# Moved matmuls in the output projection and the expert layer, and the last sums started from two fp32r terms

## The chip, the cores and the metric

The kernel runs on one core of a Trainium2 chip. The core's engines run their own instruction streams side by side: TensorE (PE in the rows; PEld are its weight loads), VectorE (DVE), ScalarE (ACT), GpSimd (POOL) and SyncE (SP, which here only issues DMAs). The metric is the device time of one execution in microseconds (us); several executions are timed and the median is taken.

## The reference

One layer of a decoder trunk on 512 tokens of width 1024, in float32: a token mixer (attention, pooling and state-space branches, merged and projected), a layer norm, then 32 experts of which each token uses two, and a second layer norm. Cut to the parts that the change touches:

```python
def layer_norm(h, g, b, eps=1e-5):
    mu = jnp.mean(hf, -1, keepdims=True)
    var = jnp.mean(jnp.square(hf - mu), -1, keepdims=True)
    return ((hf - mu) * lax.rsqrt(var + eps)).astype(h.dtype) * g + b

def moe_ffn(x, w_grp, b_grp, w_exp, b_exp, w_gate, w_up, w_down):
    p_grp = jax.nn.softmax((xf @ w_grp + b_grp).astype(jnp.float32), -1)
    ...
    w_top, e_top = lax.top_k(p_in, MOE_TOPK)
    ...
    def expert_block(args):
        xb, e = args
        h = jax.nn.silu(xb @ w_gate[e]) * (xb @ w_up[e])
        return h @ w_down[e]

    ys = lax.map(expert_block, (xs, blk_e)).reshape(P, D)
    out = jax.ops.segment_sum(ys * buf_w[:, None].astype(ys.dtype), buf_t, num_segments=T)

def reference(x, w_in, ...):
        mix = token_mixer(x, w_in[l], ...)      # ends in merged @ w_out
        x = layer_norm(DN_ALPHA * x + mix, ln1_g[l], ln1_b[l])
        ffn = moe_ffn(x, router_w_grp[l], ...)
        x = layer_norm(DN_ALPHA * x + ffn, ln2_g[l], ln2_b[l])
```

## The kernel before

The 512 tokens are four tiles `tt` of 128 rows. `out_proj` (from about 515 us) multiplies the merged branches by `w_out`, 512 output columns (a half) at a time: a first half with all four tiles (96 matmuls of `mm3`, lines 70 to 72, each fp32 product made of three fp32r ones), then for each tile the second half, the transposition of its rows (`transpose_rows`, line 1055), the norm and the routing. Inside it `router_consts` folds the norm's gain and bias into the router's weights: VectorE sums products of the router's weights with `gb`, which is loaded on ScalarE's queue (line 927), into `wsum`, and TensorE adds these over the partitions with one matmul against ones (line 938).

`moe` (from 595 us) then goes through the 32 experts in order. An expert's weights are 6 MB, in six pieces of 1 MB: two for gate, two for up, two for down. SyncE loads them (`load_piece`, line 1439) in the order gate(e), up(e), down(e-1), into a ring of 20 buffers; a piece is issued when the program order reaches it and its buffer's last reader is done. For each expert TensorE does 32 matmuls of gate and up (`gate_up`, line 1355) into one bank `mm`; `hidden` (lines 1364 to 1366) makes `th` of them on ScalarE and VectorE; `turn` transposes `th` of the expert before (line 1374) between gate and up, and `flush` calls `down` (line 1387) for it, whose result is cast and subtracted (lines 1391, 1393) into a high and a low fp32r part `y`. After each odd expert, `gather_turn` (line 1342) turns the next pair's rows and `combine` adds the pair's outputs, by 16 matmuls with a selection matrix `ot` (lines 1408, 1409; four per tile) and 8 additions on VectorE (line 1418), to `acc`, which begins as the norm's output times a constant (`residual`). `route_further` and `further_slots` work out slots for tokens beyond an expert's 64; they are wanted by `overflow`, a loop on the chip that stands ahead of expert 16 and runs as often as there are further blocks. Ahead of it, weights are loaded up to 13 pieces past the start of expert 16.

At the end, `start_tile` puts `acc` into the last sums' banks with a matmul against the identity, the last pair's outputs are added in the same banks, and `final` takes norms from them (line 1592) and writes the output. Most of TensorE's instructions are pinned in program order (`inorder`); the others are placed by a scheduler.

Of the kernel before, what the change touches and what calls it, by code (L numbers as in the profile page):

```python
# [18 lines left out]
S = 512  # L19
# [24 lines left out]
class Build:  # L44
# [869 lines left out]
    def router_consts(self, p):  # L914
# [22 lines left out]
        ps = self.bank("o")  # L937
        nc.tensor.matmul(ps[:, 0:72], ones, sm.rearrange("p i n -> p (i n)"), start=True, stop=True)
        nsg = p.tile([128, 36], F32, name="nsg")
        nc.vector.tensor_scalar(nsg, ps[:, 0:36], -1.0, None, op0=OP.mult)  # L940
        V(br, br, ps[:, 36:72], OP.add)
        return wr, nsg, br

    def out_proj(self, mh, ml):
# [11 lines left out]
        rc = self.router_consts(p)  # L956
# [16 lines left out]
        for tt in range(NT):  # L973
            evac(0, tt, accs[tt])

# [106 lines left out]

    def residual(self, t, c):

        nc = self.nc
        cs = slice(c * 512, (c + 1) * 512)
        for i, nm in enumerate(("ln1_g", "ln1_b")):
            nc.scalar.dma_start(t[:, i], dram(self.I[nm], c * 512, [[0, 128], [1, 512]]))
        nc.scalar.mul(t, t, ALPHA)
        for tt in range(NT):  # L1090
            r = self.acc[tt // 2][:, tt % 2, cs]
            self.tc.keep_in_program_order(nc.vector.tensor_tensor(r, r, t[:, 0], OP.mult))
            nc.vector.tensor_tensor(r, r, t[:, 1], OP.add)
# [215 lines left out]
    def further_slots(self, part):  # L1309
# [4 lines left out]
        if part == 0:  # L1314
            self.fps = self.bank("pt")[0:64, 0:32]
        for tt in (part * 2, part * 2 + 1):
            for i in range(2):
# [6 lines left out]
                self.inorder(nc.tensor.matmul(self.fps, rk, wo.rearrange("p a n -> p (a n)"), start=(tt == 0 and i == 0),  # L1324
                                              stop=(tt == NT - 1 and i == 1)))
        if part:
            T(self.idxo, self.fps[:, 0:16], 4096.0, None, op0=OP.add)
            for h in range(2):
                T(self.wt48[h * 64:(h + 1) * 64, 32:48], self.fps[:, 16:32], 0.5, None, op0=OP.mult)
# [81 lines left out]
    def combine(self):  # L1411

        for tt in range(NT):
            for dh in range(2):
                ps = self.bank("s" if tt % 2 else "pt")
# [3 lines left out]
        self.terms = []  # L1419
# [32 lines left out]
    def moe(self):  # L1452
        p = self.ep
# [18 lines left out]
        for e in range(E):  # L1472
            pr, odd = e // 2, e % 2
            if pr == LOOP and not odd:
# [10 lines left out]
            hT = []  # L1485
            gu = self.gate_up(xq[:, :, odd * 64:(odd + 1) * 64], self.pieces(e, 0), self.pieces(e, 1),
                              (lambda: hT.append(self.turn(pend[1]))) if pend and e > 1 else None)
            if e == 0:
                self.load_until(len(self.first))
                fetch(1, xs1)  # L1490
                self.slot_weights()
                pend = (0, self.hidden(gu, self.wt48[:, 0:1]), None)
                continue
# [3 lines left out]
            if e == 2:  # L1497
                self.slots_everywhere()
                self.further_slots(0)
                pend = (*pend[:2], self.slot_rows(self.sid[:, 0:1]))  # L1500
# [4 lines left out]
            if odd:  # L1505
# [5 lines left out]
                if self.terms:  # L1511
                    self.combine()
# [3 lines left out]
            if e == 1:  # L1516
                srt = self.route_further()
            if e == 2:
                self.further_slots(1)
                srt.close()  # L1520
            if e in (1, 2):
                self.residual(gb, e - 1)
            if odd and pr:
                ot = self.slot_rows(self.sid[:, pr:pr + 1], t=self.moe_tile() if end else None)
            pend = (e, th, ot if odd and pr else None)
        self.ahead = [self.start_tile(tt) for tt in range(2)]
        self.flush(pend, self.turn(pend[1]))
# [3 lines left out]
    def start_tile(self, tt):  # L1531

        halves = [self.bank(t) for t in (("s", "s"), ("mm", "mm"), ("mm", "pt"), ("pt", "o"))[tt]]
        for dh in range(2):
            self.nc.tensor.matmul(halves[dh], self.ident, self.acc[tt // 2][:, tt % 2, dh * 512:(dh + 1) * 512], start=True, stop=False)  # L1535
        return halves

# [222 lines left out]
```

## Time and profile before

| | us |
|---|---|
| median of 3 runs (1094.75 to 1098.54) | 1097.99 |
| the profiled execution | 1097.79 |
| its span, first to last instruction | 1096.1 |
| TensorE busy | 999.9 (91%) |
| VectorE busy | 593.6 (54%) |
| ScalarE busy | 317.0 (29%) |
| GpSimd busy | 201.1 (18%) |

The granted TensorE clock is 0.962 of full speed on average. DMA moved 256.21 MB, of which the experts' weights are the greater part. The shares are averages over stages with different limits: what an edit in one stage is worth is read from the rows of that stage.

### The profile page before, as it was taken

The page shows a single profiled execution, that of the slowest core. Times are in us where ns is not written, and L with a number is a line of the kernel's source. Part 1 is how long each engine was busy: PE and PEld are TensorE (multiplying, and loading weights), DVE is VectorE, ACT ScalarE, POOL GpSimd, SP SyncE. Part 2 cuts the span into 40 slices and gives each one's busy share as a digit, 9 for nine tenths or more (in the row PEclk, how much of TensorE's full clock was granted, in tenths as well). Part 3 has the DMA queues.
Part 4 walks back from the last instruction along what each step waited for, and adds up shares of the span by engine and source line. Part 5 has one row for each costly group of instructions (what it writes and reads, how often), then busy time and mean ns, then how long its engine had stood idle before and what let it go on. Part 6 is the DMA issues. An engine that isn't in the chain of part 4 may idle for free. (4 is left out here: it accounts for less than half of the span.)

```text
span 1096.1 us, 15867 instructions
## 1 busy us (share of the span) xinstructions
PE 999.9 (91%) x6189; PEld 698.7 (64%) x6189; DVE 593.6 (54%) x1427; ACT 317.0 (29%) x662; POOL 201.1 (18%) x179
## 2 busy tenths in 40 slices
PE   7969988999989999999698879999996999999994
PEld 6956676778778777888585455555552655555552
DVE  7992667474788784253255384444444244444436
ACT  4322222334556564232122121111110111111112
POOL 5410213334111223453112000000000000000003
PEclk9995999999999899999899989999998899999997
DMA  6701442225111112735415999999998999999992
GB/s 201 225 1 23 98 82 77 78 71 165 38 39 40 39 39 66 281 115 198 158 74 215 409 382 418 418 418 419 418 419 360 403 418 418 418 418 418 419 375 77
DMA packets 79821, 256.21 MB, mean 234 GB/s; under 512 B 16544, under 2 KB 43712, under 8 KB 55168
## 3 DMA queue, kind: packets, MB, share of 16 engines
q1 hardware_dynamic: 68064, 245.56, 57.4%
q10 hardware_dynamic: 8944, 3.59, 2.1%
q0 software_dynamic: 2736, 6.03, 1.5%
q8 instruction: 49, 0.80, 0.3%
q14 instruction: 28, 0.23, 0.1%
HBM read 254.40 MB, written 4.69 MB: 236 GB/s over the span
## 5 line engine op out<-in xcount | busy, mean ns | idle before, releaser
L1355 PE MATMUL ps_mm<-w,xq 128*64 128x256 f32 x1296 | 148.3, 381 | 0.0
L102 POOL TENSOR_TENSOR whl<-w,whl 128x1024 fp32r<-128x1024 f32 (+3 forms) x41 | 94.7, 2318 | 278.7 <-ACT whl L113 237.9
L1355 PEld LDWEIGHTS ps_mm<-w,xq 128*64 128x64 f32 x1296 | 91.2, 137 | 53.3 <-issue 8.6
L72 PE MATMUL ps_mm<-xh,whl 128*128 128x512 f32 x288 | 115.8, 402 | 0.0
L71 PE MATMUL ps_mm<-xl,whl 128*128 128x512 f32 x288 | 115.4, 401 | 0.0
L70 PE MATMUL ps_mm<-xh,whl 128*128 128x512 f32 x288 | 115.2, 400 | 0.0
L1365 DVE SCALAR_TENSOR_TENSOR th<-th,ps_mm 128x256 f32<-128x256 f32 x32 | 13.5, 421 | 161.2 <-ACT th L1364 161.2
L1393 DVE TENSOR_TENSOR y<-ps_o,y 64x512 fp32r<-64x512 f32 x60 | 41.3, 689 | 86.7 <-ACT y L1391 79.3
L1335 POOL DMA_INDIRECT xq<-zd,idx x14 | 14.0, 1003 | 389.8 <-PE ps_pt L1408 306.3
L1391 ACT CAST y<-ps_o 64x512 fp32r<-64x512 f32 x60 | 34.8, 579 | 141.7 <-issue 81.9
L1387 PE MATMUL ps_o<-w,hT 128*64 128x512 f32 x288 | 69.6, 608 | 0.0
L72 PEld LDWEIGHTS ps_mm<-xh,whl 128*128 128x128 f32 x288 | 54.7, 190 | 11.0 <-issue 0.8
L71 PEld LDWEIGHTS ps_mm<-xl,whl 128*128 128x128 f32 x288 | 54.8, 190 | 10.3
L70 PEld LDWEIGHTS ps_mm<-xh,whl 128*128 128x128 f32 x288 | 54.6, 189 | 10.4 <-issue 0.9
L113 ACT CAST whl<-w 128x1024 fp32r<-128x1024 f32 (+3 forms) x56 | 54.7, 989 | 13.5 <-PE ps_mm L72 13.4
L1355 PE MATMUL ps_mm<-rc,xq 128*64 128x256 f32 x384 | 46.8, 393 | 0.0
L1387 PEld LDWEIGHTS ps_o<-w,hT 128*64 128x64 f32 x288 | 21.4, 139 | 36.0 <-issue 33.0
L1364 ACT ACTIVATE th<-ps_mm 128x256 f32<-128x256 f32 x32 | 12.3, 383 | 104.8 <-PE ps_mm L1355 104.8
L1355 PE MATMUL ps_mm<-rd,xq 128*64 128x256 f32 x368 | 42.2, 381 | 0.0
L1355 PEld LDWEIGHTS ps_mm<-rc,xq 128*64 128x64 f32 x384 | 27.9, 142 | 17.6 <-issue 4.9
L1418 DVE TENSOR_TENSOR acc<-acc,ps_pt 128x512 f32<-128x512 f32 x60 | 38.4, 677 | 0.0
L1418 DVE TENSOR_TENSOR acc<-acc,ps_s 128x512 f32<-128x512 f32 x60 | 38.2, 677 | 0.0
(581 smaller groups left out, 2064.4 us busy)
## 6 DMA issues: line engine op xcount, KB each, us to landing
w<-in_moe_w_up_dram SPq DMA_DIRECT2D x43, 1024.0 KB, 19.9
w<-in_moe_w_gate_dram SPq DMA_DIRECT2D x38, 1024.0 KB, 20.3
w<-in_moe_w_down_dram SPq DMA_DIRECT2D x37, 1024.0 KB, 20.0
w<-in_w_in_dram SPq DMA_DIRECT2D x17, 1024.0 KB, 5.0
rc<-in_moe_w_down_dram SPq DMA_DIRECT2D x14, 1024.0 KB, 19.9
rc<-in_moe_w_gate_dram SPq DMA_DIRECT2D x14, 1024.0 KB, 19.9
rd<-in_moe_w_down_dram SPq DMA_DIRECT2D x13, 1024.0 KB, 20.5
rd<-in_moe_w_gate_dram SPq DMA_DIRECT2D x12, 1024.0 KB, 14.6
```

Of the source, the lines that this page charges most:

```text
L70: mm(ps, a[0], b[0], start=start, stop=False)
L71: mm(ps, a[0], b[1], start=False, stop=False)
L72: mm(ps, a[1], b[0], start=False, stop=stop)
L102: (V if eng == "dve" else P)(dst, src, h, OP.subtract)
L113: pin(self.nc.scalar.copy(hv[:, :, c:c + w], src))
L1335: self.nc.gpsimd.indirect_dma_start(xs[:n], None, self.zd[:, :], bass.IndirectOffsetOnAxis(ap=idx, axis=0), bounds_check=S - 1, oob_is_err ...
L1355: self.inorder(nc.tensor.matmul(gu[hh * 64:(hh + 1) * 64, part * 256:(part + 1) * 256], xe[:, k], w[k // 4][:, k % 4, hh * 256:(hh + 1) * ...
L1365: nc.vector.scalar_tensor_tensor(th, th, 1.0, gu[:, 0:256], op0=OP.add, op1=OP.mult)
L1387: self.inorder(nc.tensor.matmul(y[dh][dh * 64:(dh + 1) * 64], hT[:, q, hh * 64:(hh + 1) * 64], wd[f // 2][:, f % 2, dh * 512:(dh + 1) * 51 ...
L1391: nc.scalar.copy(part(yh, dh), y[dh][dh * 64:(dh + 1) * 64])
L1393: nc.vector.tensor_sub(part(yl, dh), y[dh][dh * 64:(dh + 1) * 64], part(yh, dh).bitcast(F32))
L1418: self.nc.vector.tensor_tensor(a, a, ps, OP.add)
```

## The change

Five edits. (1) The matmul that sums `wsum`, with the two VectorE operations that read it, moves from inside the first half of the output projection to its end. (2) The gains for `residual` are loaded on GpSimd's queue instead of ScalarE's, earlier, and the constant factor goes into VectorE's two operations instead of a ScalarE multiply; `slots_everywhere`, `residual`, `route_further` and `further_slots` move within experts 0 to 6, and `further_slots` now adds its two parts in SBUF. (3) `combine` is split: tiles 0 and 1 between gate and up of the odd expert that follows, tiles 2 and 3 at the old place, all with other banks. (4) At the end `split_acc` makes two fp32r terms of `acc` (8 casts on ScalarE, 8 subtractions on VectorE), and `start_tile` uses two fp32r matmuls for each half instead of one fp32 matmul, in pinned order. (5) `start_tile(0)` stands ahead of the last down and `start_tile(1)` behind it.

```diff
             nc.vector.tensor_reduce(sm[:, i], t.rearrange("p k n -> p n k"), axis=AX.X, op=OP.add)
-        ps = self.bank("o")
-        nc.tensor.matmul(ps[:, 0:72], ones, sm.rearrange("p i n -> p (i n)"), start=True, stop=True)
         nsg = p.tile([128, 36], F32, name="nsg")
-        nc.vector.tensor_scalar(nsg, ps[:, 0:36], -1.0, None, op0=OP.mult)
-        V(br, br, ps[:, 36:72], OP.add)
-        return wr, nsg, br
+
+        def sums():
+            ps = self.bank("o")
+            self.tc.keep_in_program_order(nc.tensor.matmul(ps[:, 0:72], ones, sm.rearrange("p i n -> p (i n)"), start=True, stop=True))
+            nc.vector.tensor_scalar(nsg, ps[:, 0:36], -1.0, None, op0=OP.mult)
+            V(br, br, ps[:, 36:72], OP.add)
+        return (wr, nsg, br), sums
 
...
               for j in range(2)] for i in range(2)]
-        rc = self.router_consts(p)
+        rc, sums = self.router_consts(p)
 
...
             evac(0, tt, accs[tt])
+        sums()
 
...
 
+    def gains(self, t, c):
+
+        nc = self.nc
+        for i, nm in enumerate(("ln1_g", "ln1_b")):
+            nc.gpsimd.dma_start(t[:, i], dram(self.I[nm], c * 512, [[0, 128], [1, 512]]))
+
     def residual(self, t, c):
 
         nc = self.nc
         cs = slice(c * 512, (c + 1) * 512)
-        for i, nm in enumerate(("ln1_g", "ln1_b")):
-            nc.scalar.dma_start(t[:, i], dram(self.I[nm], c * 512, [[0, 128], [1, 512]]))
-        nc.scalar.mul(t, t, ALPHA)
         for tt in range(NT):
             r = self.acc[tt // 2][:, tt % 2, cs]
-            self.tc.keep_in_program_order(nc.vector.tensor_tensor(r, r, t[:, 0], OP.mult))
-            nc.vector.tensor_tensor(r, r, t[:, 1], OP.add)
+            self.tc.keep_in_program_order(nc.vector.scalar_tensor_tensor(r, r, ALPHA, t[:, 0], op0=OP.mult, op1=OP.mult))
+            nc.vector.scalar_tensor_tensor(r, t[:, 1], ALPHA, r, op0=OP.mult, op1=OP.add)
 
...
         if part == 0:
-            self.fps = self.bank("pt")[0:64, 0:32]
+            self.fsum = p.tile([64, 32], F32, name="rfs")
+        fps = self.bank("pt")[0:64, 0:32]
         for tt in (part * 2, part * 2 + 1):
...
                 T(wo[:, 1], io, bk, self.wk[:, i, tt:tt + 1], op0=OP.is_equal, op1=OP.mult)
-                self.inorder(nc.tensor.matmul(self.fps, rk, wo.rearrange("p a n -> p (a n)"), start=(tt == 0 and i == 0),
-                                              stop=(tt == NT - 1 and i == 1)))
+                self.inorder(nc.tensor.matmul(fps, rk, wo.rearrange("p a n -> p (a n)"), start=(tt % 2 == 0 and i == 0),
+                                              stop=(tt % 2 == 1 and i == 1)))
         if part:
-            T(self.idxo, self.fps[:, 0:16], 4096.0, None, op0=OP.add)
+            nc.vector.tensor_tensor(self.fsum, self.fsum, fps, OP.add)
+            T(self.idxo, self.fsum[:, 0:16], 4096.0, None, op0=OP.add)
             for h in range(2):
-                T(self.wt48[h * 64:(h + 1) * 64, 32:48], self.fps[:, 16:32], 0.5, None, op0=OP.mult)
+                T(self.wt48[h * 64:(h + 1) * 64, 32:48], self.fsum[:, 16:32], 0.5, None, op0=OP.mult)
+        else:
+            nc.vector.tensor_copy(self.fsum, fps)
 
...
 
-    def combine(self):
-
-        for tt in range(NT):
+    def combine(self, tiles=range(NT), tags=("pt", "s")):
+
+        for tt in tiles:
             for dh in range(2):
-                ps = self.bank("s" if tt % 2 else "pt")
+                ps = self.bank(tags[tt % 2])
                 self.combine_tile(ps, self.terms, tt, dh, True)
                 a = self.acc[tt // 2][:, tt % 2, dh * 512:(dh + 1) * 512]
                 self.nc.vector.tensor_tensor(a, a, ps, OP.add)
-        self.terms = []
+        if NT - 1 in tiles:
+            self.terms = []
 
...
             hT = []
+
+            def between():
+                hT.append(self.turn(pend[1]))
+                if self.terms:
+                    self.combine((0, 1), ("s", "mm"))
             gu = self.gate_up(xq[:, :, odd * 64:(odd + 1) * 64], self.pieces(e, 0), self.pieces(e, 1),
-                              (lambda: hT.append(self.turn(pend[1]))) if pend and e > 1 else None)
+                              between if pend and e > 1 else None)
             if e == 0:
                 self.load_until(len(self.first))
                 fetch(1, xs1)
                 self.slot_weights()
+                self.gains(gb, 0)
                 pend = (0, self.hidden(gu, self.wt48[:, 0:1]), None)
                 continue
             if e == 1:
                 fetch(2)
                 hT.append(self.turn(pend[1]))
-            if e == 2:
-                self.slots_everywhere()
-                self.further_slots(0)
-                pend = (*pend[:2], self.slot_rows(self.sid[:, 0:1]))
+            if e in (4, 6):
+                self.further_slots(e // 2 - 2)
+                if e == 6:
+                    srt.close()
             end = pr == pairs - 1
...
                 if self.terms:
-                    self.combine()
+                    self.combine((2, 3), ("pt", "mm"))
+                if end:
+                    self.asplit = [self.split_acc(tt) for tt in range(NT)]
                 self.y = self.ytile(end)
             if pend:
                 self.flush(pend, hT[0])
-            if e == 1:
-                srt = self.route_further()
             if e == 2:
-                self.further_slots(1)
-                srt.close()
+                self.slots_everywhere()
+                self.terms[0] = (self.slot_rows(self.sid[:, 0:1]), *self.terms[0][1:])
             if e in (1, 2):
                 self.residual(gb, e - 1)
+            if e == 1:
+                self.gains(gb, 1)
+                srt = self.route_further()
             if odd and pr:
-                ot = self.slot_rows(self.sid[:, pr:pr + 1], t=self.moe_tile() if end else None)
+                t = self.moe_tile() if end else None
+                ot = self.slot_rows(self.sid[:, pr:pr + 1], t=t)
+                if end:
+                    self.identr = t.bitcast(F32R)[:, S:S + 128]
+                    nc.scalar.copy(self.identr, self.ident)
             pend = (e, th, ot if odd and pr else None)
-        self.ahead = [self.start_tile(tt) for tt in range(2)]
-        self.flush(pend, self.turn(pend[1]))
+        hT = self.turn(pend[1])
+        self.ahead = [self.start_tile(0)]
+        self.flush(pend, hT)
+        self.ahead.append(self.start_tile(1))
         self.steady = False
...
         for dh in range(2):
-            self.nc.tensor.matmul(halves[dh], self.ident, self.acc[tt // 2][:, tt % 2, dh * 512:(dh + 1) * 512], start=True, stop=False)
+            for i, t in enumerate(self.asplit[tt]):
+                self.inorder(self.nc.tensor.matmul(halves[dh], self.identr, t[:, dh * 512:(dh + 1) * 512], start=(i == 0), stop=False))
         return halves
+
+    def split_acc(self, tt):
+
+        t = self.moe_tile().bitcast(F32R)
+        for dh in range(2):
+            cs = slice(dh * 512, (dh + 1) * 512)
+            self.split2(self.acc[tt // 2][:, tt % 2, cs], t[:, cs], t[:, D + dh * 512:D + (dh + 1) * 512])
+        return t[:, :D], t[:, D:]
 
```

The order of TensorE's instructions is compared between the two programs at three places. First, the output projection, as a difference: the names are `ps_o` the bank of the summed weights, `whl` the split `w_out`, `mh` and `ml` the two parts of the merged branches.

```order
 L72 MATMUL ps_mm<-whl,ml_4702 128x512
 L70 MATMUL ps_s<-whl,mh_4700 128x512
-L938 MATMUL ps_o<-wsum,xT 128x72
 L71 MATMUL ps_s<-whl,mh_4700 128x512
 L72 MATMUL ps_s<-whl,ml_4702 128x512
```

```order
 L71 MATMUL ps_s<-whl,mh_4701 128x512
 L72 MATMUL ps_mm<-whl,ml_4703 128x512
-L1055 MATMUL ps_pt<-ident,acc 128x128 x4
+L941 MATMUL ps_o<-wsum,xT 128x72
+L1058 MATMUL ps_pt<-ident,acc 128x128 x4
 L70 MATMUL ps_mm<-whl,mh_4700 128x512
 L71 MATMUL ps_mm<-whl,mh_4700 128x512
```

The matmul of the sums moved behind 53 matmuls of the first half, and stands now just ahead of the first transposition of the second half. Second, TensorE in the last odd expert, 31: before, from the transposition of `th` on (`w` and `rc` are weights, `xq` the expert's rows).

```order
L1374 MATMUL ps_pt<-ident,th 128x128 x2
L1355 MATMUL ps_mm<-w,xq 64x256 x8
L1355 MATMUL ps_mm<-rc,xq 64x256 x8
L1408 MATMUL ps_pt<-y,ot 128x512
L1409 MATMUL ps_pt<-y,ot 128x512
```

And now:

```order
L1384 MATMUL ps_pt<-ident,th 128x128 x2
L1418 MATMUL ps_s<-y,ot 128x512
...
L1419 MATMUL ps_mm<-y,ot 128x512
L1365 MATMUL ps_mm<-w,xq 64x256 x8
L1365 MATMUL ps_mm<-rc,xq 64x256 x8
L1418 MATMUL ps_pt<-y,ot 128x512
...
L1419 MATMUL ps_mm<-y,ot 128x512
L1397 MATMUL ps_o<-rc,hT 64x512 x4
```

Eight of the 16 combining matmuls moved from behind up to between gate and up, and the other eight, of tiles 2 and 3, end in bank `mm`, which is also the bank of gate and up. Third, TensorE at the last two downs, before, where `acc` and `ident` mark `start_tile`:

```order
L1387 MATMUL ps_o<-w,hT 64x512 x4
L1535 MATMUL ps_s<-acc,ident 128x512 x2
L1535 MATMUL ps_mm<-acc,ident 128x512
L1374 MATMUL ps_pt<-ident,th 128x128 x2
L1535 MATMUL ps_mm<-acc,ident 128x512
L1387 MATMUL ps_o<-w,hT 64x512
L1387 MATMUL ps_pt<-w,hT 64x512
```

And now, where `rd` and `rc` are the terms of `acc` and the fp32r identity:

```order
L1397 MATMUL ps_o<-w,hT 64x512 x4
L1384 MATMUL ps_pt<-ident,th 128x128 x2
L1562 MATMUL ps_s<-rd,rc 128x512 x4
L1397 MATMUL ps_o<-w,hT 64x512
L1397 MATMUL ps_pt<-w,hT 64x512
...
L1562 MATMUL ps_mm<-rd,rc 128x512 x4
```

The transposition of the last `th` comes right behind the down of expert 30, with four short matmuls between it and the last down, and tile 1's four stand behind the last down.

## Rows read from the trace of the kernel before

**Rows 1.** Windows: us, busy time by engine, granted clock, DMA share, GB/s.

```profile
524.00:540.00 16.00, 6.66 (x23) 5.16 (x22) 4.58 (x8) 1.05 (x1) 2.36 (x1) 0.68 0.56 217
640.00:660.00 20.00, 19.34 (x118) 12.52 (x116) 15.60 (x39) 4.47 (x9) 1.00 (x1) 0.90 0.96 369
660.00:829.00 169.00, 165.65 (x1136) 93.89 (x1132) 70.84 (x132) 30.89 (x69) 5.00 (x5) 1.00 1.01 418
829.00:849.00 20.00, 9.87 (x32) 4.60 (x32) 7.62 (x12) 2.28 (x5) 0.00 (x0) 0.82 0.84 347
860.00:1060.00 200.00, 196.06 (x1380) 113.33 (x1377) 78.08 (x150) 38.45 (x87) 6.00 (x6) 1.00 1.01 418
```

**Rows 2.** Timeline of SyncE's DMA issues: start, length, transfer.

```profile
629.71 13.85 SPq L1439 DMA_DIRECT2D w<-in_moe_w_up_dram  x2
...
828.47 0.33 SPq L1439 DMA_DIRECT2D rc<-in_moe_w_up_dram  x1
849.00 0.34 SPq L1439 DMA_DIRECT2D w<-in_moe_w_up_dram  x1
...
1035.97 0.33 SPq L1439 DMA_DIRECT2D rc<-in_moe_w_up_dram  x1
1038.47 0.33 SPq L1439 DMA_DIRECT2D rc<-in_moe_w_down_dram  x1
```

**Rows 3.** DMA view, 1030 to 1040 us: one issue, KB, us to landing.

```profile
rc<-in_moe_w_up_dram SPq DMA_DIRECT2D x1, 1024.0 KB, 19.9
```

**Rows 4.** SyncE's waits, 828 to 850 us: total us, times, longest.

```profile
SPq L1558 <- SPq L1558: 13.8, 6, 2.5
```

**Rows 5.** Timeline of the output projection, with the idle time before an instruction.

```profile
515.10 0.39 PE L70 MATMUL ps_mm<-whl,mh 128*128 128x512 f32 x1
...
520.53 0.39 PE L70 MATMUL ps_mm<-whl,mh 128*128 128x512 f32 x1
...
531.14 0.46 DVE L933 TENSOR_TENSOR xT<-wr,gb 128x288 f32<-128x288 f32 x1 [7.85 <-DMA rc<-in_moe_w_down_dram]
...
534.34 0.67 PE L938 MATMUL ps_o<-wsum,xT 128*128 128x72 f32 x2 [9.34 <-DVE wsum L936]
...
548.43 0.63 PE L1055 MATMUL ps_pt<-ident,acc 128*128 128x128 f32 x4
```

**Rows 6.** TensorE's waits, 600 to 700 us: total us, times, longest.

```profile
PE ps_pt L1324 <- DVE rwo L1323: 6.3, 2, 4.3
PE ps_o L1387 <- ACT hT L1375: 5.3, 1, 5.3
```

**Rows 7.** Timeline of the end, from the last up on.

```profile
1056.22 1.90 PE L1355 MATMUL ps_mm<-rc,xq 128*64 128x256 f32 x16
1058.05 0.50 PE L1408 MATMUL ps_pt<-y,ot 128*128 128x512 f32 x1
...
1059.52 0.47 DVE L1366 SCALAR_TENSOR_TENSOR th<-th,wt,ps_mm 128x256 f32<-128x256 f32 x1
...
1063.22 1.94 PE L1387 MATMUL ps_o<-rc,hT 128*64 128x512 f32 x8
...
1066.81 1.98 PE L1535 MATMUL ps_s<-acc,ident 128*128 128x512 f32 x4
1066.92 1.17 ACT L1391 CAST rd<-ps_o 64x512 fp32r<-64x512 f32 x2 [8.38 <-PE ps_o L1387]
...
1069.97 0.37 ACT L1375 COPY hT<-ps_pt 128x256 f32<-128x256 f32 x1 [1.87 <-PE ps_pt L1374]
1070.66 0.13 PEld L1387 LDWEIGHTS ps_o<-w,hT 128*64 128x64 f32 x1 [0.76 <-ACT hT L1375]
...
1073.73 0.59 PE L1387 MATMUL ps_pt<-w,hT 128*64 128x512 f32 x1
...
1076.40 1.34 DVE L1592 BATCH_NORM_STATS2 st<-ps_s 128x6 f32<-128x512 f32 x2
```

**Rows 8.** Costliest groups of the page: busy us, mean ns of one, idle before.

```profile
L1393 DVE TENSOR_TENSOR y<-ps_o,y 64x512 fp32r<-64x512 f32 x60 | 41.3, 689 | 86.7 <-ACT y L1391 79.3
```

More of the change, by code (lines that the diff above doesn't have):

```diff
@@ L1452, in moe @@
     def moe(self):
-        p = self.ep
+        nc, p = self.nc, self.ep
         self.worder, self.wt = [], []
```

## The prediction

> **What bounds the kernel now.** I read the windows of the expert layer first. From 660 to 829 us, and again from 860 to 1060 us, the DMA share is 1.01 and the rate 418 GB/s, while TensorE is busy 166 of 169 and 196 of 200 us [rows 1]. Two things are full at once, so I asked which of them the end hangs on. SyncE's issues are 2.50 us apart (1035.97 to 1038.47) [rows 2], which is 1 MB at 418 GB/s, and a piece lands 19.9 us after its issue [rows 3]. TensorE does the 16 matmuls of one piece in 1056.22 to 1058.05, which is 1.83 us [rows 7]. The second up piece of expert 31 was issued at 1035.97, so it landed at 1035.97 + 19.9 = 1055.87, and TensorE began to use it at 1056.22 [rows 7]: 0.35 us later. So at the end of the stream TensorE has just caught up with the weights. Whatever it saves in the second half of the experts can bring the end forward by 0.35 us at most; after that it waits for weights.
>
> The middle looks alike. Ahead of the overflow loop the last load is issued at 828.47 and the next only at 849.00 [rows 2]. In between SyncE waits at the loop's line, 13.8 us in six steps of at most 2.5 us [rows 4], which is the spacing of the pieces: it waits until all outstanding loads have landed, 828.47 + 19.9 = 848.4. TensorE is busy for only 9.87 of these 20 us [rows 1]. So the loop is left when the weights are there, and TensorE's time saved between expert 0 and the loop is idled away at it. From here on I count only what moves the stream of weights, and what comes behind its end.
>
> Two places do. In the output projection TensorE stands still for 9.34 us up to 534.34, because the matmul of `wsum` is ahead of the others in its queue [rows 5]; the stream starts only when buffers come free behind that work. And at 629.71 a pair of issues takes SyncE 13.85 us [rows 2], behind it the window 640 to 660 us has a DMA share of 0.96 and 369 GB/s instead of 1.01 and 418 [rows 1].
>
> **Edit 1, the sums.** TensorE went at 5.43 us for 24 matmuls before the wait (515.10 to 520.53), 0.226 us each [rows 5]. It stops at 534.34 - 9.34 = 525.00 with 53 matmuls of the first half left. Without the stop they end at 525.00 + 53 x 0.226 = 537.0, and the sums' matmul with 0.3 us (half of its 0.67, which was taken at a low clock) brings the first transposition to 537.3. Before it began at 548.43 [rows 5]. The gain is **11.1 us**: 9.34 of wait, the rest from the matmuls that ran slowly after it (the granted clock from 524 to 540 us is 0.68 [rows 1]). VectorE's own wait up to 531.14 for the load of `gb` stays [rows 5], and `wsum` is ready at 534.3 as before; TensorE comes to it at 537.0, 2.7 us later, so the wait is covered. If that load came 2.7 us later or more, the cover would be gone and the wait would be at the new place. The split of `w_out` that VectorE has queued behind that load is for the second half, which starts at 537. Behind the moved matmul are queued the transpositions and the whole second half. Bounds: 9.3 (the wait alone) to 11.4 (nothing for the sums).
>
> **Edit 2, the early experts.** TensorE waited 5.3 us for `hT`, which ScalarE copies, and 6.3 us for VectorE's part of `further_slots` [rows 6]. The gains go to GpSimd's queue, so the ScalarE multiply and its wait for that load go, and `further_slots` goes to experts 4 and 6. The two waits are TensorE's, and by the loop argument they are worth nothing themselves. What they do to the stream is the gap behind 629.71: a down piece's buffer was not free because its reader was queued on TensorE behind them. The gap cost (1.01 - 0.96) x 20 = 1.0 us by the share, and (418 - 369)/418 x 20 = 2.3 us by the rate; part of this traffic is small transfers that stay, so I take **1.2 us** and keep 1.0 and 2.3. Below nothing it can't well go: the two loads of the gains only change queue. The two fused VectorE operations of `residual` have the count of the two before. The extra copy and addition of `further_slots` (64x32) are off every path above.
>
> **Edit 3, the split combination.** 16 matmuls and 8 additions for each pair stay what they are. In the experts before the last it takes short waits of TensorE away, and by what is said above they are worth 0 to 0.35 us. At the end it costs and gives, so it goes into the next sum.
>
> **Edits 3 to 5, the end.** Let U be the landing of the second up piece of expert 31, 1055.87 before. Before, the last down ends at 1073.73 + 0.59 = 1074.32 [rows 7], U + 18.45. After, TensorE has caught up with the stream ahead of U, since 1.83 us of work meet 2.50 us of stream. The second gate piece lands at U - 5.0 and is done at U - 3.2. Then come the transposition of `th` (two 128x128 matmuls, 0.3 by an estimate from the 0.226 of one with 512 columns) and tiles 0 and 1, 8 matmuls by 0.226 = 1.8, up to U - 1.1; the first up piece to U + 0.75 and the second to U + 2.6, U + 2.7 with the end of the last matmul. `th` took from 1056.22 + 1.90 = 1058.12 to 1059.52 + 0.47 = 1059.99 [rows 7], 1.87 us, so it is there at U + 4.6, tile 2 lying beside it. Tile 3's first bank is `mm`, which gate and up still hold until `th` is made, so its four matmuls (0.9) end at U + 5.5. The down of expert 30 takes 1063.22 to 1066.81, 3.59 us, to U + 9.1; its pieces land at U + 2.5 and U + 5.0, in time. ScalarE's two casts follow with 1.17, the small copy of the identity with about 0.2 (an estimate from the 0.37 of `hT`, of which it has half the elements), and `hT` with 0.37: U + 10.9. Meanwhile the four fp32r matmuls of `start_tile(0)` wait for the copied identity at U + 10.5 and end 0.9 later, U + 11.4; before, the fp32 ones took 1.98 for the same tile [rows 7]. The last down takes 1070.66 to 1074.32, 3.66 us [rows 7], and one matmul of tile 2 stands in it, 0.23: U + 15.3. Tile 1's four matmuls stand between it and the last pair's outputs, where the first norm operation came at 1076.40, 2.08 us after the down; they lie under the 0.6 of a cast and stick out by some 0.2. So the gain is 18.45 - 15.3 - 0.2, **3.0 us**. Lower bound 0: the eight subtractions of the split take 8 x 0.69 = 5.5 us by their nearest row [rows 8], and if VectorE or ScalarE were late with them in front of `th`, the whole gain could go. Upper bound 4.0: the bank wait of tile 3 falls away. The norms and the output behind it are as they were.
>
> **The sum.** 11.1 + 1.2 + 3.0 = 15.3. The profiled execution took 1097.79, 0.2 below the median of the runs, so its time can stand for them: 1097.79 - 15.3 = **1082.5 us**. Low ends together (9.3 + 1.0 + 0) give 1087.5, high ends (11.4 + 2.3 + 4.0) 1080.1; with the runs' own spread of some 3.8 us the likeliest case has 1077 to 1089.
>
> **Rivals.** *The wait only moves.* VectorE stands until 531.14 at a load that lies in a busy queue; if that load lands later in the changed kernel, or a split of `w_out` queued behind it is late for the second half, the output projection ends where it did. For it: TensorE's new margin is only 2.7 us. Against it: nothing ahead of that load changes. Then 1.2 + 3.0 are left, 1093.6.
>
> *The end gives nothing.* The conversions are late, or the bank wait is longer: 1097.79 - 12.3 = 1085.5, inside the likeliest case's range; the change would not do what its fifth edit does in the order.
>
> *Slower: TensorE falls to the low clock.* After the change TensorE meets the weights earlier, and stands some 2.50 - 1.83 = 0.67 us at each piece. A wait of 9.34 us was followed by a granted clock of 0.68, and the stop at the loop by 0.82 [rows 1]. If the short waits did the same and the clock went to the lower of its two levels (1.2 instead of 2.4 GHz), a piece would take 3.66 us against 2.50, an expert of six pieces 22 instead of 15 us, 7 us more. The whole gain and 5.5 us more are lost with the third such expert; four give 1082.5 + 28 = 1110. Against it: TensorE is busy 98% from 860 to 1060 us with the clock at 1.00 [rows 1], and in the changed kernel it would be busy some 73% and more at each piece, with no stop longer than 0.7 us. The Trainium skill, "TensorE: Matmul & The Clock Gate", section "HAM oscillation — how this bites in real kernels", describes a kernel whose work for one weight slice is shorter than its wait for the next, and which falls back to the low clock at every slice. Here the wait is shorter than the work, so by that rule the clock stays; that is no part of the numbers above.
>
> **Chances.** Likeliest case with the second rival in it 0.86, the wait that moves 0.08, the low clock 0.06. A measurement of this kernel tells about 0.5%, 5.5 us, from no change: faster is below 1092.5, slower above 1103.5. The moved wait lies mostly inside that bound, with a part of it below, the low clock beyond. Faster 0.88, same 0.06, slower 0.06. The range that leaves out two in ten goes from 1076 to 1090.
>
> **What would show it.** After the change: no wait ahead of the sums' matmul and the first transposition at 537 to 538; SyncE's first issue behind the loop at 836 to 837, 12.3 us earlier than 849.00; the last pieces land 12.3 us earlier; TensorE waits for weights in the last pairs, with the clock at 1.00; the last down ends 15 us earlier, and from it to the end nothing changes. Wrong it would be if the loop's exit did not move with the stream, if SyncE had a new gap between 600 and 660 us, if VectorE's split stood in front of `th`, or if the clock fell ahead of 1060 us.

## The result and the profile after

The changed kernel takes **1078.58 us** in the median of four runs (1077.99 to 1082.16), the kernel before 1097.71 on the same chip: a ratio of 0.9837 with a 95% interval of 0.9809 to 0.9866, which is 15 to 21 us faster. Forecast were 1082.5 and a range of 1076 to 1090. Run once more beside three experiments on another occasion it had 0.9860 (0.9843 to 0.9876), 15 us.

The profiled execution took 1077.99 us with a span of 1076.2, and the clock's mean is 0.968. Its windows, with the columns of [rows 1]:

```profile
524.00:540.00 16.00, 16.00 (x79) 13.42 (x77) 9.81 (x15) 1.64 (x2) 2.39 (x1) 1.00 0.55 201
...
625.00:645.00 20.00, 20.00 (x144) 12.11 (x142) 14.09 (x44) 4.37 (x10) 1.05 (x1) 1.00 1.02 419
645.00:811.00 166.00, 158.64 (x1075) 92.97 (x1071) 75.14 (x141) 30.74 (x69) 5.02 (x5) 1.00 1.01 418
811.50:831.50 20.00, 0.00 (x0) 0.00 (x0) 0.00 (x0) 0.00 (x0) 0.00 (x0) 0.52 0.85 351
842.00:1042.00 200.00, 196.30 (x1379) 112.40 (x1376) 82.37 (x155) 40.92 (x91) 6.00 (x6) 1.00 1.01 418
```

The stop in the output projection is gone (16.00 of 16 us busy, clock 1.00), and the stretch behind 625 us has no hole in the DMA any more. At the loop no engine does anything for 20 us. SyncE's issues and the waits there, to compare with [rows 2] and [rows 4]:

```profile
608.96 2.83 SPq L1450 DMA_DIRECT2D w<-in_moe_w_up_dram  x2
...
811.23 0.33 SPq L1450 DMA_DIRECT2D rc<-in_moe_w_up_dram  x1
831.52 0.34 SPq L1450 DMA_DIRECT2D w<-in_moe_w_up_dram  x1
...
1018.47 0.33 SPq L1450 DMA_DIRECT2D rc<-in_moe_w_up_dram  x1
```

```profile
PE ps_s L1352 <- DMA rc<-in_moe_w_up_dram: 22.8, 1, 22.8
```

The loop is left 20.3 us after the last issue ahead of it (20.5 before), and TensorE now waits 22.8 us for it: the time it saved in front is spent here. The output projection and the first gate, for [rows 5]:

```profile
511.45 0.39 PE L70 MATMUL ps_mm<-whl,mh 128*128 128x512 f32 x1
...
533.21 0.33 PE L941 MATMUL ps_o<-wsum,xT 128*128 128x72 f32 x2
533.38 0.67 PE L1058 MATMUL ps_pt<-ident,acc 128*128 128x128 f32 x4
...
580.58 2.60 PE L1365 MATMUL ps_mm<-w,xq 128*64 128x256 f32 x22
```

The first gate of the kernel before, from its timeline:

```profile
595.56 4.75 PE L1355 MATMUL ps_mm<-w,xq 128*64 128x256 f32 x42
```

From the first matmul of the first half to the first transposition are 21.93 us, against 33.33 before: 11.4 gained, 96 matmuls at 0.227 each without a stop. And the end, for [rows 7]; the second up piece of expert 31 lands at U = 1018.47 + 19.9 = 1038.37 (19.9 as in [rows 3]):

```profile
1030.91 1.95 PE L1365 MATMUL ps_mm<-w,xq 128*64 128x256 f32 x16 [0.55 <-DMA w<-in_moe_w_gate_dram]
...
1039.37 1.90 PE L1365 MATMUL ps_mm<-rc,xq 128*64 128x256 f32 x16
...
1042.00 0.39 PE L1419 MATMUL ps_pt<-y,ot 128*128 128x512 f32 x1
1042.23 0.39 PE L1418 MATMUL ps_mm<-y,ot 128*128 128x512 f32 x1
1042.67 0.47 DVE L1376 SCALAR_TENSOR_TENSOR th<-th,wt,ps_mm 128x256 f32<-128x256 f32 x1
...
1043.26 1.94 PE L1397 MATMUL ps_o<-rc,hT 128*64 128x512 f32 x8
...
1048.04 0.30 ACT L1548 CAST rc<-ident 128x128 fp32r<-128x128 f32 x1
1048.36 0.37 ACT L1385 COPY hT<-ps_pt 128x256 f32<-128x256 f32 x1
1048.39 1.20 PE L1562 MATMUL ps_s<-rd,rc 128*128 128x512 f32 x4 [1.04 <-ACT rc L1548]
1048.44 1.38 DVE L1403 TENSOR_TENSOR rc<-ps_o,rc 64x512 fp32r<-64x512 f32 x2
1049.92 0.61 PE L1397 MATMUL ps_o<-w,hT 128*64 128x512 f32 x1 [0.34 <-issue]
...
1053.56 0.59 PE L1397 MATMUL ps_pt<-w,hT 128*64 128x512 f32 x1
...
1056.24 1.40 DVE L1627 BATCH_NORM_STATS2 st<-ps_s 128x6 f32<-128x512 f32 x2
```

The last down ends at 1053.56 + 0.59 = 1054.15, U + 15.8 instead of U + 18.45.

**Where the 19.9 us between the two spans went.** 3.7 lie ahead of the output projection (its first half starts at 511.45 instead of 515.10), where nothing was changed. 11.4 are the first half. From the first gate matmul (580.58, before 595.56) to the issue of the second up piece of expert 31 are 437.9 us instead of 440.4: 2.5. The tail from U to the last down gives 2.7. The rest, from the last down to the end and between the transposition and the first gate, takes back 0.4. The 3.7 are a matter of the clock. Windows in the attention stage, first of the kernel before, then of the changed kernel, then of the changed kernel run again (e12 below):

```profile
285.00:320.00 35.00, 31.89 (x180) 25.96 (x179) 29.37 (x85) 20.30 (x56) 4.91 (x2) 0.95 0.10 30
360.00:395.00 35.00, 34.70 (x194) 28.11 (x192) 27.51 (x95) 20.01 (x56) 3.71 (x2) 0.90 0.08 29
```

```profile
285.00:320.00 35.00, 31.88 (x187) 25.62 (x187) 30.39 (x91) 20.79 (x57) 4.92 (x2) 1.00 0.09 30
360.00:395.00 35.00, 34.69 (x205) 27.79 (x204) 30.08 (x103) 22.23 (x62) 3.72 (x2) 1.00 0.05 19
```

```profile
165.00:200.00 35.00, 31.74 (x239) 23.22 (x239) 22.40 (x33) 9.61 (x14) 12.15 (x5) 0.90 0.25 68
```

The same instructions run with the clock at its upper level in one execution and partly at the lower one in another, in one place or another: e12 has 1.00 in the first two windows, the changed kernel's first profile 1.00 in the third. The start of the first half follows it over all fourteen profiles of this document. It is 511.3 and 511.5 us in the two whose granted clock stays at its upper level from 110 us on (e2 and the changed kernel), 515.1 to 515.2 in the three that fall to the lower level in both of the first two windows (before, e7, e11), and between these in the nine that fall once. So one pair of profiles is not fit to count 3 us by its spans; stages are compared, each from its own start.

### The profile page after: what moved, and what is told of

Read it like the earlier page. It is cut to its first block, busy times and chain, and to the rows that moved or that the text cites. A ratio compares the mean times of both kernels' runs of the same rounds, so it can differ in the third digit from the quotient of the medians.

```text
span 1076.2 us, 15925 instructions
## 1 busy us (share of the span) xinstructions
PE 984.6 (91%) x6189; PEld 693.6 (64%) x6189; DVE 600.4 (56%) x1437; ACT 320.2 (30%) x669; POOL 204.1 (19%) x183
## 5 line engine op out<-in xcount | busy, mean ns | idle before, releaser
L1385 ACT COPY hT<-ps_pt 128x256 f32<-128x256 f32 x32 | 11.9, 372 | 94.2 <-PE ps_pt L1384 94.1
L1352 PE MATMUL ps_s<-ident,xq 128*128 128x128 f32 x112 | 18.0, 306 | 22.8 <-DMA rc<-in_moe_w_up_dram 22.8
## 6 DMA issues: line engine op xcount, KB each, us to landing
rd<-in_moe_w_down_dram SPq DMA_DIRECT2D x13, 1024.0 KB, 19.9
rd<-in_moe_w_gate_dram SPq DMA_DIRECT2D x12, 1024.0 KB, 19.9
```

Of the source, the lines that this page charges most:

```text
L1352: self.inorder(self.nc.tensor.transpose(banks[k // 4][:, k % 4 * 128:k % 4 * 128 + n], xs[:n, self.fk(k)], self.ident[:n, :n]))
```

## The experiments

"Stream" below is the time from the first gate matmul to the issue of the second up piece of expert 31 (440.4 us before, 437.9 after), "tail" the time from that piece's landing U to the end of the last down (18.45 before, 15.79 after), both from the trace of each run.

**One edit at a time, from the kernel before.** e1: the sums alone.

```diff
-        ps = self.bank("o")
-        nc.tensor.matmul(ps[:, 0:72], ones, sm.rearrange("p i n -> p (i n)"), start=True, stop=True)
...
         for tt in range(NT):
             evac(0, tt, accs[tt])
+        sums()
```

> Only the matmul of the sums is moved, all else is as before. If the stream of weights starts behind the output projection and carries its shift to the end, the time falls by the 11.1 us worked out for it, to 1086.6 from a median of 1097.7, and SyncE's first issue behind the loop comes 11 us earlier (counted from the start of the output projection). If the stop at the loop takes early savings away, it stays at 1097.7. Beside it: the changed kernel's profile was 4.2 us shorter ahead of 513 us, in attention, where nothing is changed, with a granted clock of 1.00 instead of 0.93 and 0.96 in two windows. If these are chance, kernels with unchanged attention show them in some executions and not in others, and times of one kernel lie 2 to 4 us apart.

1086.08 us, ratio 0.9910 (0.9894 to 0.9927): 8 to 12 us faster than the 1095.69 of before in that comparison. The early saving goes through the loop to the end, as only the first of the two theories has it.

e2: the reordering of experts 0 to 6 alone (gains on GpSimd's queue, residual, further slots), the rest as before.

```diff
-            if e == 2:
-                self.slots_everywhere()
-                self.further_slots(0)
+            if e in (4, 6):
+                self.further_slots(e // 2 - 2)
...
+                self.gains(gb, 0)
```

> Only the work of experts 0 to 6 is reordered (gains on GpSimd's queue, residual, further slots). If only the stream counts, the gain is that of the gap in SyncE's issues, 1.2 us as predicted or 2.2 us as the changed kernel's trace has it between 580 and 811 us: 1095.5 to 1096.5. If TensorE's waits of 5.3 and 6.3 us were on the path to the end, 11.6 us: 1086.

1093.25 us, 0.9982 (0.9970 to 0.9994): 0.7 to 3.3 us. TensorE's 11.6 us of waits are gone from its trace, and most of them were worth nothing. The stream takes 438.0 us. In the five kernels that keep the old order of these experts it takes 440.4 (before), 441.9 (e1), 443.0 (e3), 442.3 (e4) and 442.3 (e8): the profile that I forecast from was the best of the five. By these traces the edit is worth 2.4 to 5.0 us, 3.9 in the mean, but four of the five kernels carry other edits too, and the runs of e2 itself say 0.7 to 3.3.

e3: the two terms and the new places of tiles 0 and 1 alone. e4: the split combination alone. e8: both.

```diff
+                if end:
+                    self.asplit = [self.split_acc(tt) for tt in range(NT)]
...
-        self.ahead = [self.start_tile(tt) for tt in range(2)]
-        self.flush(pend, self.turn(pend[1]))
+        hT = self.turn(pend[1])
+        self.ahead = [self.start_tile(0)]
+        self.flush(pend, hT)
+        self.ahead.append(self.start_tile(1))
```

```diff
+                if self.terms:
+                    self.combine((0, 1), ("s", "mm"))
...
-                    self.combine()
+                    self.combine((2, 3), ("pt", "mm"))
```

> Only the two fp32r terms and the new places of the first two tiles at the end; the combination stays whole behind up. By the tail's sum the down of expert 30 ends at U + 10.9 as before, then casts, copy and hT bring the last down to U + 13.3 and its end to U + 17.1 instead of U + 18.45: 1.2 us gained, 1096.5. If the split's subtractions stand in front of th, no gain or a loss of up to 2 us.

> Only the combination is split. In the experts ahead of the last nothing can be gained but 0.35 us. At the end the down of expert 30 starts at U + 5.5 instead of U + 7.35: 1.8 us gained, 1095.9. If tiles 0 and 1 ahead of up make TensorE late for the weights, or the bank wait costs more than 0.9 us, no gain.

> The kernel before with the split combination and the two fp32r terms together (no sums moved, nothing of experts 0 to 6). Alone, the split gave U + 17.54 for the last down's end and the terms U + 17.91, against U + 18.45 before and U + 15.79 in the changed kernel. If the two need each other (the unpinned fp32 matmuls slip between the weights' matmuls of up and down when only the split is done; VectorE's eight subtractions hold up the bank of the last down when only the terms are), this one ends the last down at U + 15.8 and gains 2.7 us in the tail. If the gain came from the other edits, U + 17 or later.

e3: 1097.14 us, 1.0006 (0.9993 to 1.0019). e4: 1096.35, 1.0005 (0.9992 to 1.0019). e8: 1094.74, 0.9984 (0.9971 to 0.9997). The times of e3 and e4 can't be told from no change; what follows is read from the traces. The tails are 17.9, 17.5 and 15.79 us: alone the edits give 0.5 and 0.9, together 2.7, and the tail of e8 is the changed kernel's to 0.01 us. Why, the timelines show. With the split alone the fp32 matmuls of `start_tile`, which the scheduler places, stand between the pieces of up and of down:

```profile
1055.92 1.13 PE L1541 MATMUL ps_s<-acc,ident 128*128 128x512 f32 x2
1056.97 1.95 PE L1355 MATMUL ps_mm<-rc,xq 128*64 128x256 f32 x16
...
1060.91 1.94 PE L1387 MATMUL ps_o<-rc,hT 128*64 128x512 f32 x8
1062.78 1.12 PE L1541 MATMUL ps_s<-acc,ident 128*128 128x512 f32 x2
```

With the terms alone all sixteen combining matmuls still lie behind up, VectorE gets to its eight subtractions only at 1063.52, and the last down waits, to judge by the times, for bank `o`, which VectorE's next subtraction frees:

```profile
1063.52 4.89 DVE L279 TENSOR_TENSOR rd<-acc,rd 128x512 fp32r<-128x512 f32 x8
...
1068.34 1.38 DVE L1393 TENSOR_TENSOR rc<-ps_o,rc 64x512 fp32r<-64x512 f32 x2
...
1069.82 0.61 PE L1387 MATMUL ps_o<-w,hT 128*64 128x512 f32 x1 [1.57 <-issue]
```

The profile names no releaser for the 1.57 us, but the subtraction ends at 1069.72, 0.1 ahead of the matmul. In the changed kernel four of the eight are done ahead of `th`, and 0.34 us of this wait are left in its rows above; there too the subtraction ends 0.1 ahead of the matmul (1048.44 + 1.38 = 1049.82).

**The stop at the loop.** e5 is the changed kernel without `self.overflow()`, which leaves out the further blocks (the trace of before shows no pass of the loop). e6 loads 7 pieces ahead instead of 13. e7 puts the loop into the tail.

```diff
-                self.overflow()
```

```diff
-                held = self.worder.index((e, 0, 0)) + len(self.ring) - 7
+                held = self.worder.index((e, 0, 0)) + len(self.ring) - 13
```

```diff
-LOOP = 8
+LOOP = 16
...
         hT = self.turn(pend[1])
+        self.overflow()
         self.ahead = [self.start_tile(0)]
```

> The changed kernel without the overflow loop (it leaves out the experts' further blocks; the trace shows no pass of that loop). If the stream of weights is what the end hangs on and the stop at the loop costs the stream 10 us (79 pieces land in 207.2 us between 831.1 and 1038.4, at 2.493 us each they would take 197.0), the time falls by 9 to 10 us against the changed kernel: 1069 beside 1078.6. If the stop's price were TensorE's wait of 22.8 us, it falls by up to 20. If the end hangs on TensorE's work, nothing is gained beyond a few us.

> The changed kernel, with 7 instead of 13 pieces of expert 16 and later loaded ahead of the loop. If the loop's exit hangs on the landing of the loads issued ahead of it, the exit comes 6 pieces, 15 us, earlier, TensorE waits 8 us there instead of 22.8, and the end stays within 2 us, as the stream has as many pieces more to load behind it. If the time TensorE stands still at the loop were on the path to the end, the time falls by up to 15 us.

> The changed kernel, with the overflow loop moved behind the transposition of the last th, ahead of the first start tile; its passes redo the two terms of acc, and take their th and hT from another buffer. The stream then runs without a stop and gives the 10 us; the loop's entry stands in the tail, where all engines meet while the last pieces land: 2 to 4 us lost. 1072 beside 1078.6 for the changed kernel. If the meeting costs as much as the stop, no gain.

e5: 1078.02 us, 0.9833 (0.9807 to 0.9858), beside the changed kernel's 0.9837 no gain that can be told; the two intervals leave room for 3 us. In its trace the stream is 3.1 us shorter (434.8), not 10, and the tail is the same 15.8, so the last down ends 3.1 us earlier, counted from the first gate. My 10 had all of the DMA's time go to pieces, but the gathers and other small transfers run in the same stretch (85.9 MB were moved in it, 82.8 of them the 79 pieces); the right size can be read from the changed kernel's window at the stop, a DMA share of 0.85 for 20 us, which lacks (1.01 - 0.85) x 20 = 3.2 us. e5 has no such hole:

```profile
800.00:820.00 20.00, 15.20 (x78) 8.45 (x80) 9.96 (x18) 3.80 (x9) 1.00 (x1) 0.91 1.01 419
820.00:840.00 20.00, 20.00 (x162) 11.94 (x160) 4.36 (x10) 4.18 (x10) 1.00 (x1) 1.00 1.02 417
```

So TensorE's stand of 22.8 us at the loop costs the stream 3 us by the traces, and the stream is what the end hangs on. e6: 1080.53, 0.9861 (0.9839 to 0.9883). Its loop is left 15.0 us earlier, counted from the first gate, TensorE waits there for 7.6 us instead of 22.8, and the stream takes 438.0: the exit moves with the loads, the end doesn't.

```profile
PE ps_s L1352 <- DMA w<-in_moe_w_up_dram: 7.6, 1, 7.6
```

e7: 1079.12, 0.9835 (0.9803 to 0.9866). The stream gains the 3 us (434.7) and the tail loses 3.9: TensorE stands for 2.98 us at the loop, and works slowly behind it: the granted clock from 1050 to 1057 us is 0.51, and a matmul of the last down takes 1.06 to 1.12 us instead of 0.59.

```profile
1050.79 2.07 PE L1563 MATMUL ps_s<-rd,rc 128*128 128x512 f32 x4 [2.98 <-DVEq L1594]
1052.80 1.12 PE L1397 MATMUL ps_o<-w,hT 128*64 128x512 f32 x1
```

**Which of the early waits held the stream, and another order of the end.** All from the changed kernel: e10 has the further slots in expert 2 again, e11 the gains' loads on ScalarE's queue in `residual`; e9 does the down of expert 30 ahead of expert 31's gate. e12 is the changed kernel itself.

```diff
-            if e in (4, 6):
-                self.further_slots(e // 2 - 2)
+            if e == 2:
+                self.further_slots(0)
```

```diff
-            nc.gpsimd.dma_start(t[:, i], dram(self.I[nm], c * 512, [[0, 128], [1, 512]]))
+            nc.scalar.dma_start(t[:, i], dram(self.I[nm], c * 512, [[0, 128], [1, 512]]))
...
+        self.gains(t, c)
...
-                self.gains(gb, 0)
...
-                self.gains(gb, 1)
```

```diff
-            self.worder += dn + gu if e == 2 * LOOP else gu + dn
+            self.worder += dn + gu if e in (2 * LOOP, E - 1) else gu + dn
...
+            if last:
+                self.y = self.ytile(True)
+                self.flush(pend, self.turn(pend[1]))
```

> The changed kernel with the two parts of further slots back in expert 2, ahead of and behind its down. If TensorE's wait for VectorE in them is what held the buffer that SyncE waited for, the long gap in SyncE's issues (2.5 us apart in the changed kernel there) comes back with 5 us or more, and the first issue behind the loop comes 1 to 3 us later counted from the first gate matmul. If it was the wait for the gains, no gap.

> The changed kernel with the loads of the gains back on ScalarE's queue, issued in residual. If ScalarE's queue with these loads made TensorE wait for hT and held the buffer, a gap in SyncE's issues comes back and the first issue behind the loop is 1 to 3 us later counted from the first gate matmul. As the ScalarE multiply that waited for the loads is gone, I expect 0 to 0.5 us.

> The changed kernel with the down of expert 30, and its two pieces, ahead of gate and up of expert 31. The stream ends with the same number of pieces at V = U + 10 of the changed kernel; the second up piece lands at V - 5, up ends at V - 3.1, th is there at V - 1.2, hT at V - 0.3, the last down runs from V or shortly before its last piece to V + 4. The changed kernel's last down ends at U + 15.8 = V + 5.8. So 1.5 to 2 us gained, 1076.8 beside 1078.6. If the end is set by VectorE's subtractions of the split or by the small copies instead of the down of expert 30, nothing is gained.

> The changed kernel once more, on the same chip as the three above: 1078.6 if nothing differs, 1077 to 1082 with the dips of the clock in attention. It is the measure for the three: what is explained there by the dips must show as a dip in the profile ahead of 513 us.

e12: 1081.28 us, 0.9860 (0.9843 to 0.9876). Its profile differs from the first one of the same kernel in the output projection too:

```profile
530.50 0.46 DVE L933 TENSOR_TENSOR xT<-wr,gb 128x288 f32<-128x288 f32 x1 [8.58 <-DMA rc<-in_moe_w_down_dram]
...
531.38 2.97 POOL L102 TENSOR_TENSOR whl<-rc,whl 128x1024 fp32r<-128x1024 f32 x1 [6.34 <-ACT whl L113]
...
532.01 2.65 DVE L934 TENSOR_TENSOR wr<-wr,gb 128x288 f32<-128x288 f32 x1
...
535.96 0.41 PE L941 MATMUL ps_o<-wsum,xT 128*128 128x72 f32 x2 [0.31 <-DVE wsum L936]
...
537.60 0.75 PE L1058 MATMUL ps_pt<-ident,acc 128*128 128x128 f32 x4 [1.22 <-DVE acc L962]
```

VectorE waits for the load of `gb` for 8.58 us instead of 7.42. Its product of `wr` and `gb` (L934) then starts while GpSimd is at a split of `w_out`, and takes 2.65 us instead of 0.45. So TensorE waits for `wsum` and again for `acc`, which VectorE makes after it, and the first half takes 23.9 us to the first transposition instead of 21.9. Of the nine profiles with the moved sums four are like this (e5, e9, e10, e12; 23.4 to 23.9 us): in these the product starts behind the start of GpSimd's split, in the other five ahead of it, with 0.45 us. In the five profiles with the sums at the old place the product takes 0.45 us too, and GpSimd comes to this split only behind the stop (544.32 us in the kernel before, 29.2 us from the start of the first half; 17.7 in the nine with the sums moved). That the split makes the product long is read from these profiles; no experiment was made for it.

e10: 1078.98, 0.9839 (0.9826 to 0.9852). e11: 1079.43, 0.9847 (0.9833 to 0.9861). Neither is slower than e12; their streams are 438.0 and 438.5 against 437.9. In e10 the wait and the gap in the issues did come back, and the DMA went on beside them:

```profile
PE ps_pt L1331 <- DVE rwo L1330: 8.5, 1, 8.5
```

```profile
611.49 12.68 SPq L1450 DMA_DIRECT2D w<-in_moe_w_up_dram  x2
```

```profile
610.00:620.00 10.00, 1.30 (x10) 0.72 (x6) 9.42 (x43) 0.38 (x1) 1.12 (x2) 0.65 1.02 419
620.00:630.00 10.00, 9.86 (x64) 6.05 (x66) 6.54 (x25) 2.33 (x4) 0.00 (x0) 0.84 1.01 417
```

A gap of 12.7 us is covered by the loads in flight, since a piece takes 19.9 us to land. In the kernel before, a gap of nearly the same length cost 2.5 us, and there the issues ahead of it were late as well: the 15th issue behind the first gate stood at 32.4 us, in e10 at 26.0 and in the changed kernel at 25.9. What was left of the queue shows in the time to landing of the first piece issued behind the gap, in the kernel before (643 to 646 us) and in e10 (623 to 628 us):

```profile
w<-in_moe_w_up_dram SPq DMA_DIRECT2D x1, 1024.0 KB, 4.9
```

```profile
w<-in_moe_w_up_dram SPq DMA_DIRECT2D x1, 1024.0 KB, 11.5
```

e11 has the lateness alone: its 15th issue stands at 34.6 us, behind a gap of 5.9 us, and the DMA share stays at 1.01 to 1.02. So neither delay alone ran the queue dry, and undoing either of the two edits costs 0.6 us at most; the kernel before, and the others with the old order, have both.

e9: 1083.42, 0.9878 (0.9856 to 0.9900), which is not faster than e12. Two downs in a row share the one bank `o`: TensorE waits 2.3 us for VectorE, its 16 matmuls then take 5.35 instead of 3.6 us, and later it waits 1.8 us for the copied identity, which is queued behind ScalarE's casts of `acc`. Its last down ends 2.4 us later than e12's, counted from the first gate.

```profile
PE ps_o L1397 <- DVE y L1403: 2.3, 1, 2.3
PE ps_s L1568 <- ACT rc L1554: 1.8, 1, 1.8
```

None of the versions tried is clearly faster than the changed kernel.

## Why the prediction was right

*What bounds.* Right at both places. The stream decides: e6 and the trace of e5 show it, and e2 shows that 11.6 us of TensorE's waits bring 0.7 to 3.3. In the changed kernel's last pair TensorE waits 0.55 us for a gate piece and starts it on arrival, as the sum of the tail assumed.

*The sums, 11.1 us.* Right in the main: 11.4 between the two profiles, 9.6 between the medians of e1. In the first profile `wsum` was ready at 530.1 and TensorE came at 533.2: the cover that I gave as 2.7 us was 3.1. In e12's profile the cover was gone and the gain 9.5, still inside my bounds of 9.3 to 11.4.

*The early experts, 1.2 us.* The mechanism was right, the size taken was low: 2.5 between the two profiles, a little above my upper bound of 2.3, which came from a hole in one window (640 to 660 us) of one execution. Of the two readings of that hole, by the share 1.0 and by the rate 2.3, the rate was the nearer. The runs of e2 (0.7 to 3.3) can't tell 1.2 from 2.5. And I put the gap down to both of TensorE's waits. By e10 the one for `further_slots` brings it alone, by e11 the gains' loads make the issues late, and each of these alone is hidden under the loads in flight.

*The end, 3.0 us.* 2.7 from U to the last down, less 0.3 behind it. Several terms were off and partly cancel. Tile 3's matmuls did not wait for a bank: the first stands 0.23 us behind its neighbour and ahead of the operation that finishes `th`, and the down of expert 30 starts 0.6 us earlier than I had it. Against that, the last down waits 0.34 us, to judge by the times for bank `o` from VectorE, which I left out; the four start matmuls take 1.2 us instead of 0.9; and the last down with tile 2's matmul in it takes 4.23 us (1049.92 to 1054.15) instead of 3.66 + 0.23. That the sum came out within 0.6 us of the gain is in part luck. The lower bound's mechanism, VectorE late with the split's subtractions, was real, but at bank `o` and not ahead of `th`, and it fired in e3.

*The rivals.* The wait that moves did not come in the first profile, where nothing stands ahead of the sums, but it came in part in e12, e5, e9 and e10, and took 1.5 to 2.0 us. The condition that I gave for it, a load 2.7 us later, asked too much: in e12 the load came only 1.2 us later, and the other 2.2 us of the cover went into VectorE's product beside GpSimd's split. I had said that nothing changes ahead of `wsum`; but without the stop GpSimd comes to that split 11.6 us earlier, counted from the start of the first half. The low clock did not come: from 842 to 1042 us the clock is 1.00, though TensorE waits for pieces at its end, 0.55 us beside 1.95 of work. The Trainium skill, "TensorE: Matmul & The Clock Gate", section "HAM oscillation — how this bites in real kernels", describes a kernel whose wait for the next slice is longer than its work on one, and whose clock falls at every slice. This trace has waits shorter than the work, and agrees as far as it goes.

*The sum.* 15.3 predicted. The first profile gives 11.4 + 2.5 + 2.7 - 0.4 = 16.2 for what was changed, e12's 9.5 + 2.5 + 2.7 - 0.4 = 14.3. The other 3.7 us of the first pair belong to the clock in attention. That part was in no step of the prediction but in its range, by the spread of the runs. The medians themselves lie 19 us apart on the first occasion and 15 on the second, a spread wider than either of the two smaller terms.

## What to carry to other kernels

Ask first which stretch can be left only when transfers have landed: time saved ahead of such a place counts only if it brings the transfers forward, and a stand of 22.8 us at a full stop cost the stream 3. A gap in the issues is free as long as the loads in flight outlast it, so two small delays in a row can cost what neither does alone. A wait taken out also lets other engines start earlier: GpSimd's split came to lie beside VectorE's product, and in four of nine profiles the cover was gone. Edits of one chain (where matmuls stand, when an engine gets to its conversions, which bank comes free) are to be tried together as well as singly: 0.5 and 0.9 us became 2.7.

## What was not expected of the hardware

TensorE's clock fell to the lower level for some microseconds in attention in twelve of the fourteen profiles, and not always at the same place, while TensorE was busy for 90% of these windows and more (0.95 and 0.90 in the windows of before, 1.00 in the changed kernel's, 0.90 at another place in e12). In the two profiles compared here the stretch with the low clock took 3.7 us more. Executions of one kernel differ by 4 us and more (1077.99 to 1082.16 for the changed kernel, 1094.18 to 1100.69 for the kernel before in 29 executions). What sets the clock off at one place or the other is open: it wasn't tried.

A VectorE product of 0.45 us (128x288 elements) took 2.65 in each of the four profiles in which it began during a GpSimd split of 2.5 to 3.0 us, and 0.45 in the five in which it began ahead of it.
